# Transformer layer in split fp32: wide products on a [high|low] operand, loads of x between the weight loads, wider empty products

## The chip, the cores and the metric

The kernel runs on one core of a Trainium2 chip. The metric is the device time of one execution in microseconds; of several runs the median is given. TensorE multiplies (its products read a stationary tile of 128 columns and stream a moving operand of up to 512), VectorE, ScalarE and GpSimd (POOL) work element by element, and the queues of SyncE (SP), ScalarE and GpSimd issue DMA transfers.

## The reference

One decoder layer on 256 tokens of width 2048: a hybrid mixer (a windowed attention with sinks and a native sparse attention), a cross-attention to 256 memory tokens, a squared-ReLU MLP, each with a residual and a layer norm.

```python
h = x @ w_in                                  # 2048 x 7216
(q_a, k_a, v_a, q_b, k_c, v_c, k_s, v_s, k_w, v_w, g_nsa, g_merge) = jnp.split(h, offsets, axis=-1)
y_a = swa_sink_attention(...); y_b = nsa_attention(...)
mix = (sigmoid(g_a) * (y_a @ w_branch_swa) + sigmoid(g_b) * (y_b @ w_branch_nsa)) @ w_mix_out
h = layer_norm(DN_ALPHA * x + mix, ln1_g, ln1_b)
xa = memory_cross_attention(h, mem, xa_w_q, xa_w_kv, xa_w_o)
h = layer_norm(DN_ALPHA * h + xa, ln2_g, ln2_b)
ff = jnp.square(jax.nn.relu(h @ mlp_w1)) @ mlp_w2       # 2048 -> 8192 -> 2048
out = layer_norm(DN_ALPHA * h + ff, ln3_g, ln3_b)
```

## The kernel before

All large matmuls are computed in a split form: each fp32 operand is written as a high part (rounded by the cast to fp32r) and a low part (the rest), and a product is high by high, high by low and low by high, three TensorE products into one sum. Activations are kept transposed, 16 tiles k of 128 features by 256 tokens, as two tensors, one of high parts and one of low parts (`xth`/`xtl` for x, `mth`/`mtl` for the merged mixer, `meth`/`metl` for memory, `h1th`, `h2th` and their low parts after the norms).

The weights come in *chunks* of 512 KB (1024 columns by 128 partitions), a list that `run_chunks` goes through in order. `emit_load` issues a chunk's DMAs on the SP queue into one of five `raw` buffers, `emit_splits` makes the high part `h` on ScalarE (line 168) and the low part `l` on VectorE (line 169), up to three chunks ahead, and the chunk's `mm` issues the products. Between chunks, `side.phase` lets side jobs (attention heads, transpositions, norms) take one step on TensorE ("pe") or on the others ("ev"). A block is the set of chunks that adds into the same PSUM banks; after its last chunk `post` issues the copies that empty the banks (`evac`). Blocks have two forms:

- `block_x` (activations stationary, weights moving, 512 columns): `mm_x`, lines 201 to 208. The gates, the branches, the mixer output, the second MLP matmul (`mlp_w2`).
- `block_w` (weights stationary, 256 tokens moving): `mm_w`, lines 216 to 219, three products 256 wide for each 128 columns of weight. The two query blocks of `w_in` (1024 columns each), the keys of the memory, the queries of the cross-attention (512 each) and the first MLP matmul `mlp_w1` (8 blocks of 1024 columns). Two 128-column results lie in one bank. Blocks use the four banks "acc"; in the first MLP matmul every other block uses four others (`alt`).

The first 16 chunks (`make_c`, key/value stage) are mixed: 432 value and gate columns as `mm_x`, five 128-column key groups as `mm_w`. Their columns lie apart in `w_in`, so each chunk is five DMAs (`kv_loads`). x itself is loaded in columns: 0 to 256 and 256 to 512 on SP around the first chunk, the rest as three loads of 512 columns from the GpSimd queue, after four small tables; `x_side` transposes 256 columns (line 1215) after each of the first chunks. Behind the key/value stage come the swa query block with eight small chunks of the compression MLP between its chunks (`make_cmp`), then the nsa query block; `compress` (lines 541 to 573) is the rest of the compression MLP, a chain of small steps on VectorE and TensorE. After a query block `evac_q` copies the banks to `qraw`, from where `stack_q` makes the operands of the heads.

`keep_warm` issues products of a zero tile that nobody reads; it is called once, with 20 products of 128 columns, in `after_wo`, just ahead of the norm that precedes the MLP.

## Time and profile before

| | |
|---|---|
| median of 3 runs | 1442.91 us (1441.77 to 1443.74) |
| profiled execution | 1444.05 us, span 1442.3 us |
| busy | PE 98%, VectorE (DVE) 61%, ScalarE (ACT) 49%, POOL 12% |
| products (MATMUL) | 8732 |
| HBM read | 264.97 MB, 185 GB/s over the span |
| stages, about | key/value 7 to 68 us, queries to 196, gates, branches, mixer to 597, cross-attention to 708, first MLP matmul to 1081, second to 1427, last norm to 1442 |

The busy time of an engine is the union of its instructions. A product shows its whole way through the array, so the next one starts before it ends; the distance from start to start is what a train of products costs. In a timeline, brackets give the idle time of the engine before the instruction and what ended it.

### The profile page before, as it was taken

To read this page: it belongs to the slowest core of one execution; us is meant where nothing else is said; L and a number is where in the kernel's file an instruction comes from. 1 tells how busy PE (TensorE), PEld (TensorE's weight loads), DVE (VectorE), ACT (ScalarE), POOL (GpSimd) and SP (SyncE) were. 2 spreads that over 40 slices of the span, in tenths; PEclk is the share of its full clock that TensorE was granted. 3 is DMA by queue.
4 is the path that set the end of the run, shared out by engine and by line. 5 is a ranking of instruction groups with operands and counts; after the bars stand their busy time and mean duration, and the time that the engine had idled before them with its cause. 6 is when DMAs were issued, how large, how long until landed. Compare 5 with 4: busy or idle time off the path is not lost.

```text
span 1442.3 us, 22448 instructions
## 1 busy us (share of the span) xinstructions
PE 1412.6 (98%) x8732; PEld 1275.6 (88%) x8732; DVE 875.2 (61%) x1323; ACT 712.0 (49%) x1098; POOL 174.5 (12%) x165
## 2 busy tenths in 40 slices
PE   7999999999999999999999999999999999999996
PEld 6999988888888888899899999999998888888885
DVE  3577887888546466675854444444446555665556
ACT  3465776677444444454444444344445544544452
POOL 3002221221001010130201111011101000000002
PEclk9999999999999999999999999999999999999998
DMA  8765555454766575574355555665657666566552
GB/s 232 228 209 186 161 150 172 146 149 132 248 192 186 190 292 184 164 239 144 132 180 186 180 184 178 190 182 184 183 183 250 193 197 191 176 212 195 192 193 84
DMA packets 96282, 268.58 MB, mean 186 GB/s; under 512 B 9344, under 2 KB 32592, under 8 KB 95408
## 3 DMA queue, kind: packets, MB, share of 16 engines
q1 hardware_dynamic: 93344, 254.71, 56.5%
q0 software_dynamic: 2832, 12.45, 2.5%
q8 instruction: 68, 1.11, 0.3%
q14 instruction: 38, 0.31, 0.1%
HBM read 264.97 MB, written 2.15 MB: 185 GB/s over the span
## 4 chain that ended last, share of the span: by engine, by line
PE 66%; issue 25%; DVE 5%; ACT 2%; POOL 1%; DMA 1%; SPq 0%; ACTq 0%; DVEq 0%; POOLq 0%
PE acc L208 22%; PE acc L216 11%; PE acc L218 11%; PE acc L219 11%; DVE l L169 2%; PE acc L201 1%; PE acc L203 1%; PE acc L202 1%; DMA raw<-in_w_in_dram 1%; PE pt L662 1%; DVE p L635 1%; PE tr L337 0%; PE hid L528 0%; PE ntr L955 0%; PE o L671 0%
## 5 line engine op out<-in xcount | busy, mean ns | idle before, releaser
L169 DVE TENSOR_TENSOR l<-raw,h 128x1024 fp32r<-128x1024 f32 (+2 forms) x469 | 590.5, 1263 | 474.5 <-ACT h L168 466.3
L168 ACT CAST h<-raw 128x1024 fp32r<-128x1024 f32 (+2 forms) x469 | 490.2, 1048 | 534.6 <-PE acc L208 255.8
L216 PE MATMUL acc<-h2th,h 128*128 128x256 f32 x1024 | 291.3, 284 | 0.0
L218 PE MATMUL acc<-h2tl,h 128*128 128x256 f32 x1024 | 290.7, 284 | 0.0
L219 PE MATMUL acc<-h2th,l 128*128 128x256 f32 x1024 | 290.6, 284 | 0.0
L216 PEld LDWEIGHTS acc<-h2th,h 128*128 128x128 f32 x1024 | 197.6, 193 | 0.0
L218 PEld LDWEIGHTS acc<-h2tl,h 128*128 128x128 f32 x1024 | 197.5, 193 | 0.0
L219 PEld LDWEIGHTS acc<-h2th,l 128*128 128x128 f32 x1024 | 197.5, 193 | 0.0
L208 PE MATMUL acc<-l,ah 128*128 128x512 f32 x476 | 146.6, 389 | 0.0
L208 PE MATMUL acc<-h,ah 128*128 128x512 f32 x476 | 146.5, 389 | 0.0
L208 PE MATMUL acc<-h,al 128*128 128x512 f32 x476 | 146.5, 389 | 0.0
L208 PEld LDWEIGHTS acc<-l,ah 128*128 128x128 f32 x476 | 89.3, 188 | 18.6
L208 PEld LDWEIGHTS acc<-h,al 128*128 128x128 f32 x476 | 89.3, 188 | 18.6
L208 PEld LDWEIGHTS acc<-h,ah 128*128 128x128 f32 x476 | 89.3, 188 | 18.5
L216 PE MATMUL acc<-xth,h 128*128 128x256 f32 x336 | 97.5, 290 | 0.1
L219 PE MATMUL acc<-xth,l 128*128 128x256 f32 x336 | 96.7, 288 | 0.0
L218 PE MATMUL acc<-xtl,h 128*128 128x256 f32 x336 | 96.7, 288 | 0.0
L208 PE MATMUL acc<-h,xth 128*128 128x512 f32 (+1 forms) x252 | 81.2, 394 | 3.5 <-ACT h L168 3.5
L1148 POOL TENSOR_TENSOR a<-relu 128x512 f32<-128x512 f32 x32 | 44.3, 1412 | 314.6 <-ACT relu L1146 314.6
L208 PE MATMUL acc<-l,xth 128*128 128x512 f32 (+1 forms) x252 | 79.7, 388 | 0.6 <-DVE l L169 0.6
L208 PE MATMUL acc<-h,xtl 128*128 128x512 f32 (+1 forms) x252 | 79.5, 387 | 0.0
L216 PEld LDWEIGHTS acc<-xth,h 128*128 128x128 f32 x336 | 66.5, 198 | 0.6 <-ACT gt L483 0.2
(304 smaller groups left out, 2139.8 us busy)
## 6 DMA issues: line engine op xcount, KB each, us to landing
raw<-in_mlp_w_dram SPq DMA_DIRECT2D x256, 512.0 KB, 4.1
raw<-in_w_in_dram SPq DMA_DIRECT2D x96, 512.0 KB, 3.6
raw<-in_w_mix_out_dram SPq DMA_DIRECT2D x32, 512.0 KB, 4.2
raw<-in_w_branch_swa_dram SPq DMA_DIRECT2D x16, 512.0 KB, 3.6
raw<-in_w_branch_nsa_dram SPq DMA_DIRECT2D x16, 512.0 KB, 3.6
raw<-in_xa_w_kv_dram SPq DMA_DIRECT2D x16, 512.0 KB, 4.4
raw<-in_w_in_dram SPq DMA_DIRECT2D x48, 128.0 KB, 2.8
tbias<-udram POOLq DMA_DIRECT2D x8, 512.0 KB, 4.9
```

What stands on the lines that cost most here:

```text
L168: nc.scalar.copy(h[:, c0:c1], raws[c][:, c0:c1])
L169: nc.vector.tensor_sub(l[:, c0:c1], raws[c][:, c0:c1], fp(h[:, c0:c1]))
L201: nc.tensor.matmul(a, lhsT=xh(s), rhs=h[:, c0:c1], start=first, stop=False)
L202: nc.tensor.matmul(a, lhsT=xh(s), rhs=l[:, c0:c1], start=False, stop=False)
L203: nc.tensor.matmul(a, lhsT=xl(s), rhs=h[:, c0:c1], start=False, stop=last)
L208: nc.tensor.matmul(acc[s, b], lhsT=lhs(s), rhs=rhs[:, c0:c1], start=False, stop=False)
L216: nc.tensor.matmul(a, lhsT=h[:, c], rhs=xh, start=first and (t % 2 == 0 if opens is None else t in opens), stop=False)
L218: nc.tensor.matmul(a, lhsT=h[:, c], rhs=xl, start=False, stop=False)
L219: nc.tensor.matmul(a, lhsT=l[:, c], rhs=xh, start=False, stop=last and (t % 2 == 1 if closes is None else t in closes))
L635: nc.vector.tensor_tensor_reduce(p[:, c:c + w], lg[:, c:c + w], tbias[n.u][:, h, :w][:, ::-1], 1.0, -3e38, OP.add, OP.max, mx[:, i:i + 1])
L662: nc.tensor.transpose(pt[:, i * P:(i + 1) * P], p[:, b * P:(b + 1) * P], ident)
L1148: nc.gpsimd.tensor_mul(box["a"][k // KD][:, k % KD:k % KD + 2, :], two(r), two(r))
```

## The change

1. The high and low parts of a transposed activation now lie beside each other, [k][high|low][256 tokens], in two tiles of eight k each (class `Parts`); `both(k)` is a 512-column operand. The slots of the operands and of `qraw`, `yt` are renumbered accordingly.
2. `block_b` takes the place of `block_w` for the query blocks, the memory keys, the cross-attention queries and 14 half blocks of the first MLP matmul (its first 1024 columns stay `block_w`). Blocks are 512 columns wide, a chunk holds two k. Per 128 columns and k there is one product 512 wide (high weight by [high|low]) and one 256 wide (low weight by high). Each result tile fills a bank, whose halves `halves` adds (ScalarE copy, then VectorE add). In the MLP the square of the ReLU goes from POOL to VectorE.
3. The key/value chunks are three DMAs, 816 columns in one piece, and their split is in three parts (four for the first chunk), which also reorder the columns. x comes in pieces of 256 columns, the first on ScalarE's queue, the others between the chunks on SP; the small tables come on SP behind chunks 5 to 7.
4. `keep_warm` products are 512 wide. There are 5 ahead of the first transpositions and 4 behind them, and 8 instead of 20 before the last norm but one. `x_side` pauses one chunk between transpositions from the third on; `small_start` starts four steps later.

```diff
+class Parts:
+    def __init__(self, *tiles):
+        self.tiles = list(tiles)
+    def part(self, i, k0, k1):
+        return self.tiles[k0 // 8][:, k0 % 8:(k1 - 1) % 8 + 1, i, :]
+    def __call__(self, k):
+        t = self.tiles[k // 8][:, k % 8]
+        return t[:, 0, :], t[:, 1, :]
+    def both(self, k):
+        return self.tiles[k // 8][:, k % 8].rearrange("p i s -> p (i s)")
...
-                nc.tensor.matmul(ps[:, :P], lhsT=idle, rhs=idle, start=True, stop=True)
+                nc.tensor.matmul(ps.rearrange("p (a n) -> p a n", a=4), lhsT=idle,
+                                 rhs=idle.unsqueeze(1).to_broadcast([P, 4, P]), start=True, stop=True)
...
-            for c0, c1 in ((512, ch.n), (0, 512)) if c == 0 else ((0, ch.n),):
-                nc.scalar.copy(h[:, c0:c1], raws[c][:, c0:c1])
-                nc.vector.tensor_sub(l[:, c0:c1], raws[c][:, c0:c1], fp(h[:, c0:c1]))
+            for src, dst in ch.parts:
+                nc.scalar.copy(dst(h), src(raws[c]))
+                nc.vector.tensor_sub(dst(l), src(raws[c]), fp(dst(h)))
...
+    def block_b(w, n0, rhs, evac, tags=("acc",) * 4, pre=None):
+        box = {}
+        for k0 in range(0, KD, 2):
+            def mm(h, l, k0=k0):
+                if k0 == 0:
+                    box["t"] = [bank(tag, "acc") for tag in tags]
+                for a in range(2):
+                    k = k0 + a
+                    for t, o in enumerate(box["t"]):
+                        c = slice((4 * a + t) * P, (4 * a + t + 1) * P)
+                        nc.tensor.matmul(o, lhsT=h[:, c], rhs=rhs.both(k), start=k == 0, stop=False)
+                        nc.tensor.matmul(o[:, :S], lhsT=l[:, c], rhs=rhs(k)[0], start=False, stop=k == KD - 1)
...
+    def halves(dst, t, scale=None):
+        if scale is None:
+            nc.scalar.copy(dst, t[:, S:])
+            nc.vector.tensor_add(dst, t[:, :S], dst)
...
-    load_x(0, 256)
+    nc.scalar.dma_start(out=xraw[:, :, :S], in_=x[:, :S].rearrange("(s p) n -> p s n", p=P))
...
-    for c in range(512, D, 512):
-        load_x(c, c + 512, nc.gpsimd)
...
+        own = [(lambda r: r[:, 128:944], rows[:, COL_KC:COL_KC + 816]),
+               (lambda r: r[:, 0:128], rows[:, COL_KA:COL_KA + 128]),
+               (lambda r: r[:, 944:1072], rows[:, COL_VA:COL_VA + 128])]
+        pieces = {1: (1,), 2: (2,), 3: (3,), 4: (4,), 6: (5,), 8: (6,), 10: (7,)}.get(k, ())
+        more = [x_piece(m) for m in pieces] + small.get(k, [])
+        more = [(lambda r, t=t: t, src) for t, src in more]
+        return more + own if k == 1 else own + more
...
-    block_w(w_in, COL_QA, 1024, xk, evac_qa)
+    block_b(w_in, COL_QA, xk, lambda tiles: evac_q(0, 0, tiles))
+    evac_first.add(len(chunks) - 1)
+    block_b(w_in, COL_QA + 512, xk, evac_qa)
...
-    block_w(xa_w_kv[0], 0, 512, mek, evac_t("kt", None))
+    block_b(xa_w_kv[0], 0, me, evac_t("kt", None))
...
-        keep_warm(20, "mi")
+        keep_warm(8, "mi")
...
+    def evac_b(f):
+        def evac(tiles):
+            for b, t in enumerate(tiles):
+                r = box["pc"].tile([P, S], F32, tag="sum", name="sum", bufs=3)
+                halves(r, t)
+                k = 4 * f + b
+                nc.vector.scalar_tensor_tensor(box["a"][k // KD][:, k % KD, :], r, 0.0, r, op0=OP.max, op1=OP.mult)
...
-    for f in range(8):
-        block_w(mlp_w1[0], 1024 * f, 1024, hk, evac_a(f), tags=alt if f % 2 else ("acc",) * 4)
+    block_w(mlp_w1[0], 0, 1024, hk, evac_a(0))
+    for f in range(2, 16):
+        block_b(mlp_w1[0], 512 * f, hk, evac_b(f), tags=("acc",) * 4 if f % 2 else alt)
...
+    keep_warm(5, "mi")
+    for g in transpose_pairs(xraw, xk, range(1), "pt"):
         pass
+    keep_warm(4, "mi")
```

The SP queue at the start of the program, before (`raw_130`, `raw_137` are the buffers of chunks 0 and 1; a wait on DMAHW is one for an earlier load of the queues):

```order
L353 DMA xraw_88<-in_x_dram 128x2x256
L151 DMA raw_130<-in_w_in_dram 128x2x128
L151 DMA raw_130<-in_w_in_dram 128x256
L151 DMA raw_130<-in_w_in_dram 128x2x128
L151 DMA raw_130<-in_w_in_dram 128x128
L151 DMA raw_130<-in_w_in_dram 128x176
L353 DMA xraw_88<-in_x_dram 128x2x256
L151 DMA raw_137<-in_w_in_dram 128x2x128
L151 DMA raw_137<-in_w_in_dram 128x256 [waits DMAHW0_49]
L151 DMA raw_137<-in_w_in_dram 128x2x128 [waits DMAHW1_49]
```

and after the change, where `raw_116`, `raw_120`, `raw_125` are chunks 0, 1 and 2 (the first piece of x is now on ScalarE's queue):

```order
L170 DMA raw_116<-in_w_in_dram 128x816
L170 DMA raw_116<-in_w_in_dram 128x128 x2
L170 DMA xraw_88<-in_x_dram 128x2x256
L170 DMA raw_120<-in_w_in_dram 128x816
L170 DMA raw_120<-in_w_in_dram 128x128 x2
L170 DMA raw_125<-in_w_in_dram 128x816 [waits DMAHW0_49]
L170 DMA raw_125<-in_w_in_dram 128x128 [waits DMAHW1_49]
L170 DMA raw_125<-in_w_in_dram 128x128 [waits DMAHW2_49]
L170 DMA xraw_88<-in_x_dram 128x2x256 [waits DMAHW3_49]
```

Chunk 0 is no longer behind the first piece of x, the second piece stands ahead of chunk 1, the third behind chunk 2; the five loads of a chunk are three.

TensorE at the end of the swa query block and the start of the nsa query block, before (`hidt` is a step of the compression MLP, `acc_754` the last bank of the old block, `acc_1412` the first of the new one):

```order
L216 MATMUL acc_754<-xth_89,h_1291 128x256
L218 MATMUL acc_754<-xtl_90,h_1291 128x256
L219 MATMUL acc_754<-xth_89,l_1292 128x256
L549 MATMUL hidt_1387<-early_92 128x32 [waits Activation_49,Pool_49]
L549 MATMUL hidt_1387<-early_92 128x32
L549 MATMUL hidt_1388<-early_92 128x32 [waits DVE_49,Pool_49]
L549 MATMUL hidt_1388<-early_92 128x32
L216 MATMUL acc_1412<-xth_89,h_1305 128x256 [waits Activation_49]
L218 MATMUL acc_1412<-xtl_90,h_1305 128x256
L219 MATMUL acc_1412<-xth_89,l_1306 128x256
L216 MATMUL acc_1412<-xth_89,h_1305 128x256
```

and after the change (`xt1_90` and `xt0_89` hold the [high|low] pairs of k 8 to 15 and 0 to 7):

```order
L307 MATMUL acc_1042<-xt1_90,h_1240 128x512
L308 MATMUL acc_1042<-xt1_90,l_1241 128x256
L307 MATMUL acc_1043<-xt1_90,h_1240 128x512
L308 MATMUL acc_1043<-xt1_90,l_1241 128x256
L612 MATMUL hidt_1323<-early_92 128x32 [waits Activation_49,Pool_49]
L612 MATMUL hidt_1324<-early_92 128x32 [waits DVE_49,Pool_49]
L307 MATMUL acc_1348<-xt0_89,h_1254 128x512 [waits DVE_49]
L308 MATMUL acc_1348<-xt0_89,l_1255 128x256
L307 MATMUL acc_1349<-xt0_89,h_1254 128x512 [waits DVE_49]
L308 MATMUL acc_1349<-xt0_89,l_1255 128x256
L307 MATMUL acc_1350<-xt0_89,h_1254 128x512 [waits DVE_49]
```

Three 256-wide products have become a 512-wide and a 256-wide one, and the new block's first product of each bank waits for VectorE, where it waited for ScalarE on the first bank; the banks follow each other every second product instead of every sixth.

TensorE at the start of the program, after the change (before, its first rows were the four transpositions `tr` and then line 201's products of chunk 0):

```order
L141 MATMUL warm_140<-idle_69 128x512 [waits DVE_49]
L141 MATMUL warm_140<-idle_69 128x512 x4
L387 MATMUL tr_146<-ident_71,xraw_88 128x128 [waits DMAHW0_49,Pool_49]
L387 MATMUL tr_146<-ident_71,xraw_88 128x128 x3
L141 MATMUL warm_153<-idle_69 128x512 [waits PE_49]
L141 MATMUL warm_153<-idle_69 128x512 x3
L566 MATMUL acc_191<-h_158,xt0_89 128x432 [waits Activation_49]
L567 MATMUL acc_191<-h_158,xt0_89 128x432 [waits DVE_49]
```

Empty products stand ahead of the first transpositions and between them and chunk 0.

## Rows read from the trace of the kernel before

**Rows 1.** The page's busy times: engine, busy us, share of the span, instructions.
```profile
PE 1412.6 (98%) x8732; PEld 1275.6 (88%) x8732; DVE 875.2 (61%) x1323; ACT 712.0 (49%) x1098; POOL 174.5 (12%) x165
```
**Rows 2.** TensorE's groups by shape: line, engine, operation, shapes, count, busy us, mean ns.
```profile
L216 PE MATMUL acc<-h2th,h 128*128 128x256 f32 x1024 | 291.3, 284 | 0.0
L216 PE MATMUL acc<-xth,h 128*128 128x256 f32 x336 | 97.5, 290 | 0.1
L216 PE MATMUL acc<-meth,h 128*128 128x256 f32 x64 | 18.5, 289 | 0.0
L216 PE MATMUL acc<-h1th,h 128*128 128x256 f32 x64 | 18.1, 283 | 0.0
```
**Rows 3.** First MLP matmul: us, busy (x) PE, PEld, DVE, ACT, POOL, clock, DMA, GB/s.
```profile
830.00:930.00 100.00, 100.00 (x836) 100.00 (x835) 43.02 (x36) 41.02 (x43) 11.12 (x8) 1.00 0.60 182
```
**Rows 4.** Timeline of PE (start, us, operation), in the first and the second MLP matmul.
```profile
801.07 0.28 PE L219 MATMUL acc<-h2th,l 128*128 128x256 f32 x1
801.19 0.28 PE L216 MATMUL acc<-h2th,h 128*128 128x256 f32 x1
...
1200.52 0.61 PE L208 MATMUL acc<-h,al 128*128 128x512 f32 x2
1201.88 0.61 PE L208 MATMUL acc<-h,al 128*128 128x512 f32 x2
```
**Rows 5.** Timeline of PE at the last key/value chunk, 432 columns followed by 256.
```profile
66.34 0.36 PE L203 MATMUL acc<-h,xtl 128*128 128x432 f32 x1
66.54 0.28 PE L216 MATMUL acc<-xth,h 128*128 128x256 f32 x1
66.66 0.28 PE L218 MATMUL acc<-xtl,h 128*128 128x256 f32 x1
```
**Rows 6.** Timeline at the start: first product, split and products of chunk 1, chunk 2.
```profile
7.34 0.73 PE L201 MATMUL acc<-h,xth 128*128 128x432 f32 x1 [2.50 <-ACT h L168]
...
16.03 1.08 ACT L168 CAST h<-raw 128x1072 fp32r<-128x1072 f32 x1 [8.22 <-DMA raw<-in_w_in_dram]
...
17.17 0.73 PE L208 MATMUL acc<-h,xth 128*128 128x432 f32 x1 [3.50 <-ACT h L168]
...
23.74 0.44 PE L208 MATMUL acc<-h,xth 128*128 128x432 f32 x1
```
**Rows 7.** Stretches of 2 us at the start, columns as in rows 3.
```profile
0.00:2.00 2.00, 0.00 (x0) 0.00 (x0) 0.25 (x4) 1.26 (x1) 1.39 (x8) 1.00 0.04 12
...
10.00:12.00 2.00, 2.00 (x10) 1.97 (x10) 0.00 (x0) 0.00 (x0) 0.73 (x1) 1.00 1.02 355
...
20.00:22.00 2.00, 2.00 (x10) 1.94 (x10) 0.21 (x1) 0.00 (x0) 0.00 (x0) 0.50 0.87 219
```
**Rows 8.** Timeline at the end of the swa query block: copies out of banks, next block.
```profile
119.89 0.37 ACT L541 COPY early<-hid 128x256 f32<-128x256 f32 x1
...
121.11 0.59 ACT L310 COPY qraw<-acc 128x512 f32<-128x512 f32 x1
121.15 0.42 DVE L542 COPY early<-hid 128x256 f32<-128x256 f32 x1
...
123.23 0.39 PE L216 MATMUL acc<-xth,h 128*128 128x256 f32 x1
```
**Rows 9.** Timeline of DVE at the end of the key/value stage.
```profile
69.30 0.56 DVE L323 TENSOR_TENSOR vs<-acc,vs 128x384 fp32r<-128x384 f32 x1 [1.07 <-ACT vs L322]
69.78 0.68 DVE L486 COPY early<-acc 128x512 f32<-128x512 f32 x1
```
**Rows 10.** TensorE's waits: who waited for whom, us in total, times, longest.
```profile
PE kvc L570 <- DVE early L561: 1.7, 1, 1.7
```
**Rows 11.** The norm ahead of the MLP: the empty products, then the stretch from 710 us.
```profile
702.22 2.34 PE L123 MATMUL warm<-idle 128*128 128x128 f32 x20
...
710.00:712.00 2.00, 2.00 (x11) 2.00 (x10) 1.47 (x3) 2.00 (x3) 1.08 (x2) 0.50 0.00 0
```

164 lines of the change are left out of this document (87 added, 77 removed).

## The prediction

> **What bounds the kernel now.** I read the busy table first, then the groups by shape, then TensorE's own order of time, and last the stretches where it stands still. TensorE is busy for 98% of the span [rows 1]; as busy says little for pipelined products, I took the distance from start to start. A product 256 columns wide starts 0.12 us after the one before it, and over 100 us of the first MLP matmul 836 of them run, with VectorE busy for 43 us of the 100 and ScalarE for 41 [rows 3, 4]. In the second MLP matmul, six products 512 columns wide go from 1200.52 to 1201.88, 0.2267 us each [rows 4]. At the full clock of 2.4 GHz, 256 and 512 columns alone would take 0.1067 and 0.2133 us, so both widths carry the same 0.0133 us on top: it goes with the product, not with the columns. Nearly all of the span is such a train; the engine really waits at three places only: the start, the little compression MLP at 130 us, and the norm at 705 us. So a change pays either in the number of products or in one of these places.
>
> **Part 1: wide products.** A 128-column weight tile against 256 tokens was three products of 256 columns (high by high, high by low, low by high). The change makes two: high by [high|low], 512 wide, and low by high. By the pitches a triple goes from 3 x 0.120 = 0.360 to 0.2267 + 0.120 = 0.3467 us, 13.3 ns less. How many triples: h2 had 1024, of which the first 1024 columns of w1 (8 tiles x 16 k = 128) keep the old form, leaving 896; the two query blocks have 16 tiles x 16 = 256 of the 336 on x, the other 80 being key/value products that stay; memory keys and cross-attention queries have 64 each [rows 2]. Together 1280, and 1280 x 13.3 ns = **-17.0 us**. No row shows the two widths in strict alternation; the nearest is a 432-wide product followed by 256-wide ones, where the steps are 0.20 and 0.12 us [rows 5], that is 432/2.4 GHz = 0.18 plus 0.02, then 0.1067 plus 0.013. The bounds are therefore 7 ns less (the step after the wide one is 0.20 instead of 0.193) and 13.3 ns a triple: -8.5 to -17 us. I take the upper end, since the wide products here are the 512 shape that already runs at 0.2267.
>
> The Trainium skill, "TensorE: Matmul & The Clock Gate", section "Back-to-back issue gap", speaks against this part: it gives an isolated gap of N/2.4 + 2.5 ns, so that a product saved is worth 2.5 ns and the whole part only 3.2 us. The pitches here disagree with it (13.3 ns at both widths), and the measurement decides.
>
> **Part 2: handing banks back.** The price of the new form is the end of a block. Half sums now lie side by side in a bank, so each 128-column tile needs a ScalarE copy (0.37 us for 256 columns) and a VectorE add (0.42) before its bank is free [rows 8]. Before, a bank was complete well ahead of the block's end: the copy of the first bank began at 121.11 and the next block's first product ran at 123.23 without a wait. Now a tile is complete only 4, 3, 2, 1 pairs before the end, 1.04 us for the first; its release takes about 0.2 + 0.37 + 0.15 + 0.42 = 1.15 us (0.2 and 0.15 are my estimates of the handshakes), and the other three follow at 0.42 where the products come at 0.35. That is some 0.3 us of waiting per end, if both engines are free, about 1.5 if a 1.2 us split is in front. In the first MLP matmul blocks alternate between two sets of four banks, so it hits no block but the last (the second matmul opens on the same four): 0.5. Ends on the same banks: first to second half of the swa queries has a compression chunk between (0); swa to nsa queries 0.5; half to half of the nsa queries 0.8; nsa queries to gates 0.3; memory keys to values and cross-attention queries to values 0.4 each. At the end of the key/value stage the second and third bank come free through VectorE ops that end at 69.85 and 70.46 [rows 9]; the first query block used them at its seventh and thirteenth product, 0.72 and 1.44 us in, and now wants them at 0.35 and 0.69: +1.2. Sum **+4.1 us**, bounds +1.5 and +9. The compression MLP then waits on VectorE (1.7 us there now [rows 10]) behind four adds of 0.42 instead of two copies of 0.6: **+0.6**, bounds 0 and +1. The extra adds in the first MLP matmul (8 ops of some 0.42 per 22 us, the squares having left POOL) are hidden: VectorE has 57% free there [rows 3]; if the cover failed, it would be 3 us for each of 14 blocks.
>
> **Part 3: the start.** Before, TensorE's first product runs at 7.34, but chunk 1 waits for its loads: ScalarE begins its split at 16.03, the products at 17.17; TensorE had stood still since 13.7, and the granted clock goes down to 0.50 (1.2 GHz), and chunk 2 starts at 23.74 [rows 6, 7]. In that time all of x and chunks 0 to 2 came in together. The change sends x in 256-column pieces between the chunks on one queue. A chunk is 128 x 1072 x 4 B = 0.55 MB, a piece 0.26 MB; nothing moves in the first 2 us, then 219 to 355 GB/s [rows 7]. The first piece and chunk 0 (0.81 MB) are in at 4.3 to 5.7, and the first product, behind transposition and a split in four pieces, runs at about 7.0. Chunk 1 and its piece (1.62 MB in all) are in at 6.6 to 9.4; chunk 2 and the third piece (2.43 MB) at 8.8 to 13.1. Chunk 0 then takes 3.0 us at the full clock (0.1067 + 0.013 for 15 products, 0.19 for 6) and 5.4 at half. Nine empty 512-wide products are set around the first transpositions, so TensorE is nearly always busy from 1 us on; I take half of chunk 0 as still slow: it ends at 11.2, four transpositions (0.4), chunk 1 from 11.6 to 14.6, four more, chunk 2 at 15.0. **-8.7 us** against 23.74; bounds: all fast, 13.9 (-9.8); loads at 219 GB/s and the clock late, 17.7 (-6.0). Splits in three pieces cost ScalarE and VectorE some 0.4 us more per chunk, hidden in 3 us; the later pieces and small tables come in while the same products run. The queue's own waits are for a load eight back, as before.
>
> **Part 4: the 20 empty products** before the last norm (2.34 us) become 8 wide ones (8 x 0.227 = 1.8): 0, as the transposition after them waits for the norm. The clock falls there now, to 0.50 at 710 [rows 11]; if it stays up, the products from 708 to 712 run at 0.12 instead of 0.21: -2 us, kept for the range.
>
> **Sum.** -17.0 + 4.1 + 0.6 - 8.7 = -21.0 us. The profiled execution took 1444.05 (span 1442.3), giving 1423.0; it lies 1.1 above the median of the three runs, 1442.91, so the forecast is **1422.0 us**. A difference of 0.2% (2.9 us) is about what a measurement can tell from none.
>
> **The rivals.** *The start stays.* The loads, not their order, bound it, and chunk 2 still begins near 23.7: 1442.9 - 17.0 + 4.7 = 1430.6. For it: 219 GB/s around 20 us; against: chunks 0 to 2 with three pieces are 2.4 MB, where before all of x (2.1 MB) was under way with them, 3.7 in all. 10%. *The products save little.* The fixed part belongs to the switch between widths or to the weights, and a triple stays near 0.358: 1442.9 - 3 + 4.7 - 8.7 = 1436. Against it stand two equal fixed parts at two widths. 5%. The rule of the Trainium skill given above would make it come out this way. Both at once, the change does nothing: 1442.9 - 3 + 4.7 = 1445, or 1443 with a better clock. 3%. *Slower: the narrow product cannot cover the next weights.* A weight load shows as 0.19 us and is hidden behind products that all have one width; if, in the alternation, the load behind each 256-wide product surfaced, the triple would be 0.2267 + 0.193 = 0.42 us, 60 ns more than now, and 1280 x 60 = 77 us: 1442.9 + 77 + 4.7 - 8.7 = 1516. It decides from 0.363 us a triple on, where it eats parts 2 and 3. Against it: the 256-wide train has its loads hidden at 0.12. 3%.
>
> **How the numbers follow.** The forecast, both gains, has 79%; its own range is 1415 (start 13.9, cheap ends, clock kept at the norm) to 1428 (start -6, ends +9 and some of part 1 lost). Taking in the rival of the start, the range is 1415 to 1431. Faster: 79 + 10 + 5 = 94, less 1 for a product rival with dear ends: 0.93. Same 0.04, slower 0.03.
>
> **What would show it.** In the new profile: 512- and 256-wide products of the first MLP matmul in pairs 0.347 us apart, some 575 products in 100 us; that matmul some 12 us shorter (896 x 13.3 ns); chunk 2 of the key/value stage at about 15 us, at the full clock; waits of products on VectorE's adds of a few tenths at each end on the same banks, 1.5 at the first. Wrong would be: a pair at 0.36 or more; chunk 1 still waiting for a load after 12 us; VectorE's splits ending TensorE's waits in the query blocks.

## The result and the profile after

The changed kernel takes 1430.35 us (median of 4 runs, 1429.42 to 1431.72), the kernel before, beside it, 1442.72 (1441.77 to 1443.74): a ratio of 0.9915, 95% interval 0.9898 to 0.9932. It is faster by 12.4 us. That lies inside the range of 1415 to 1431, at its edge; the forecast was 1422.0, so the gain is 8.4 us short of it. The forecast's own range ended at 1428, and 1430.35 is outside of that; the stretch up to 1431 had been taken in for the case that the start stays as it was, which did not come about. That the time lies inside is luck. The profiled execution is the quickest of the four, 1429.42 us with a span of 1427.6.

Busy times of the page of the changed kernel, and its groups of products in the first MLP matmul (line, engine, operation, names, shapes, count, busy us, mean ns). They answer to [rows 1, 2]:
```profile
PE 1400.0 (98%) x7449; PEld 1200.6 (84%) x7449; DVE 917.6 (64%) x1487; ACT 723.9 (51%) x1178; POOL 130.0 (9%) x123
...
L307 PE MATMUL acc<-h2t,h 128*128 128x512 f32 x896 | 316.6, 399 | 0.0
L308 PE MATMUL acc<-h2t,l 128*128 128x256 f32 x896 | 251.6, 281 | 0.0
```
There are 1283 fewer products, 1280 of them by the triples counted ahead and 3 by the empty products, and TensorE is still busy for 98%. What a product costs is not in these rows. It is in the stretch that answers to [rows 3] (us, then busy and count of PE, PEld, DVE, ACT, POOL, clock, DMA share, GB/s):
```profile
830.00:930.00 100.00, 100.00 (x568) 86.76 (x567) 56.07 (x69) 42.93 (x54) 0.00 (x0) 1.00 0.64 188
```
There are 568 products in 100 us, where the forecast wanted some 575. TensorE's order of time (start, us, operation), against [rows 4], shows the same from start to start:
```profile
830.07 0.40 PE L307 MATMUL acc<-h2t,h 128*128 128x512 f32 x1
830.31 0.28 PE L308 MATMUL acc<-h2t,l 128*128 128x256 f32 x1
830.43 0.40 PE L307 MATMUL acc<-h2t,h 128*128 128x512 f32 x1
830.66 0.28 PE L308 MATMUL acc<-h2t,l 128*128 128x256 f32 x1
```
Wide to narrow takes 0.23 or 0.24 us, narrow to wide 0.11 or 0.12. Over the stretch from 900 to 1050 us the mean distance from one wide product to the next is 353.3 ns: six products take 241, 120, 236, 113, 233 and 117 ns, 1060 ns for three pairs, and this pattern repeats without a fault. The old triple was 360.0, the forecast 346.7. Half of the 13.3 ns is there.

The start answers to [rows 6]:
```profile
1.06 2.50 PE L141 MATMUL warm<-idle 128*128 128x512 f32 x5 [1.06 <-DVE rowmask L147]
5.19 1.08 PE L387 MATMUL tr<-ident,xraw 128*128 128x128 f32 x4 [1.63 <-DMA xraw<-in_x_dram]
...
7.78 0.55 PE L566 MATMUL acc<-h,xt 128*128 128x432 f32 x1
8.14 0.39 PE L567 MATMUL acc<-h,xt 128*128 128x432 f32 x1
8.37 0.36 PE L566 MATMUL acc<-h,xt 128*128 128x432 f32 x1
8.56 0.35 PE L567 MATMUL acc<-h,xt 128*128 128x432 f32 x1
...
11.28 0.44 PE L227 MATMUL acc<-h,xt 128*128 128x432 f32 x1
...
14.65 0.44 PE L227 MATMUL acc<-h,xt 128*128 128x432 f32 x1
```
Chunk 1 waits for nothing, and chunk 2 starts at 14.65 instead of 23.74 (forecast 15.0). The clock is seen in the steps: 0.36 us for 432 columns (7.78 to 8.14) is 1.2 GHz, 0.19 (8.37 to 8.56) is 2.4. Waits of TensorE between 120 and 240 us (who waited for whom, us in total, times, longest), against [rows 10]:
```profile
PE kvc L633 <- DVE early L624: 3.0, 1, 3.0
PE o L737 <- DVE ptl L373: 1.4, 5, 0.3
PE o L736 <- ACT pth L372: 0.8, 2, 0.6
PE acc L220 <- DVE qraw L321: 0.8, 1, 0.8
```
In the kernel before, the second and third of these were 0.3 and nothing, the last nothing. But its compression MLP had a second wait, which is gone:
```profile
PE kvc L573 <- DVE early L564: 0.9, 1, 0.9
```
So TensorE waited 2.6 us there before (1.7 and 0.9) and waits 3.0 now. At the norm ahead of the MLP, two stretches (us, PE busy and count, clock, DMA share, GB/s), against [rows 11]: first the kernel before, then the changed one.
```profile
696.00:712.00 16.00, 14.32 (x75) 0.80 0.29 99
```
```profile
696.00:712.00 16.00, 13.40 (x107) 1.00 0.30 92
```

Put together by stage, from the first product of a stage to that of the next, in us:

| stage | before | changed | difference | forecast |
|---|---|---|---|---|
| to the first query product | 68.53 | 60.20 | -8.3 | -8.7 |
| first query block, to the compression MLP | 62.41 | 63.29 | +0.9 | |
| on to the first product on an attention output | 116.26 | 116.53 | +0.3 | |
| (both query stages) | 178.67 | 179.82 | +1.2 | 0.0 |
| on to the first MLP matmul | 460.81 | 459.73 | -1.1 | -0.9 |
| first MLP matmul | 373.26 | 366.29 | -7.0 | -11.9 |
| second MLP matmul and last norm | 361.0 | 361.6 | +0.6 | +0.5 |

The last column is the forecast's own terms, sorted by stage: -3.4 for 256 triples and +3.4 of waits in the queries, -1.7 and +0.8 in the cross-attention, -11.9 for 896 triples. They sum to its -21.0; the measured ones to -14.6, the difference of the two spans. The medians lie 2 us closer: the profiled execution of before is 1.3 us above the median that it is compared by, that of the changed kernel 0.9 below its own. Two stages are off: the first MLP matmul by 5 us, the queries by 1, and by more at an equal clock (see `e2_old_products`).

### The profile page after: what moved, and what is told of

It reads as the page before. It is cut to its first block, busy times and chain, and to the rows that moved or that the text cites. A ratio compares the mean times of both kernels' runs of the same rounds, so it can differ in the third digit from the quotient of the medians.

```text
span 1427.6 us, 19988 instructions
## 1 busy us (share of the span) xinstructions
PE 1400.0 (98%) x7449; PEld 1200.6 (84%) x7449; DVE 917.6 (64%) x1487; ACT 723.9 (51%) x1178; POOL 130.0 (9%) x123
## 4 chain that ended last, share of the span: by engine, by line
PE 64%; issue 26%; DVE 6%; ACT 2%; POOL 1%; DMA 0%; ACTq 0%; DVEq 0%; POOLq 0%
PE acc L227 22%; PE acc L307 18%; PE acc L308 9%; DVE l L188 2%; PE acc L235 2%; PE acc L237 1%; PE acc L238 1%; PE acc L220 1%; PE acc L221 1%; PE acc L222 1%; PE pt L728 1%; POOL res L1010 1%; PE tr L387 1%; DVE res L1009 1%; ACT h L187 0%
## 5 line engine op out<-in xcount | busy, mean ns | idle before, releaser
L188 DVE TENSOR_TENSOR l<-raw,h 128x1024 fp32r<-128x1024 f32 (+4 forms) x501 | 587.2, 1182 | 412.2 <-ACT h L187 406.0
L187 ACT CAST h<-raw 128x1024 fp32r<-128x1024 f32 (+4 forms) x501 | 493.5, 994 | 491.5 <-PE acc L227 253.5
L307 PE MATMUL acc<-h2t,h 128*128 128x512 f32 x896 | 316.6, 399 | 0.0
L308 PE MATMUL acc<-h2t,l 128*128 128x256 f32 x896 | 251.6, 281 | 0.0
L307 PEld LDWEIGHTS acc<-h2t,h 128*128 128x128 f32 x896 | 168.4, 188 | 41.9
L308 PEld LDWEIGHTS acc<-h2t,l 128*128 128x128 f32 x896 | 169.3, 189 | 0.0
L227 PE MATMUL acc<-h,xt 128*128 128x512 f32 (+1 forms) x504 | 143.5, 389 | 0.0
L227 PEld LDWEIGHTS acc<-h,xt 128*128 128x128 f32 x504 | 93.0, 188 | 16.3
L307 PE MATMUL acc<-xt,h 128*128 128x512 f32 x256 | 91.9, 400 | 1.4 <-ACT gt L538 1.4
L227 PE MATMUL acc<-l,xt 128*128 128x512 f32 (+1 forms) x252 | 79.2, 386 | 0.0
```

The costliest lines, as they stand in the source:

```text
L187: nc.scalar.copy(dst(h), src(raws[c]))
L188: nc.vector.tensor_sub(dst(l), src(raws[c]), fp(dst(h)))
L227: nc.tensor.matmul(acc[s, b], lhsT=lhs(s), rhs=rhs[:, c0:c1], start=False, stop=False)
L307: nc.tensor.matmul(o, lhsT=h[:, c], rhs=rhs.both(k), start=k == 0, stop=False)
L308: nc.tensor.matmul(o[:, :S], lhsT=l[:, c], rhs=rhs(k)[0], start=False, stop=k == KD - 1)
```

## The experiments

Each kernel is the changed one but for the edit shown (two start from the tile-outer kernel, and say so). Ratios are to the kernel before, with 95% intervals. These reach some 2 us to either side, so the medians alone do not settle a difference of 1 or 2 us between two kernels; where one is read here, it rests on the stages, of which each kernel has one profile.

### The start and the products apart

`e2_old_products` undoes the products and keeps the start:
```diff
-    block_w(mlp_w1[0], 0, 1024, hk, evac_a(0))
-    for f in range(2, 16):
-        block_b(mlp_w1[0], 512 * f, hk, evac_b(f), tags=("acc",) * 4 if f % 2 else alt)
+    for f in range(8):
+        block_w(mlp_w1[0], 1024 * f, 1024, hk, evac_a(f), tags=alt if f % 2 else ("acc",) * 4)
```
and in the same way for the queries, the keys and the cross-attention queries, with the old numbers of two small buffers.

> All blocks that the change made wide get the old three products of 256 columns again, with the old copies out of the banks; the start, the order of loads, the operand's layout and the empty products stay as changed. My theory: the start alone is worth 9.1 us (the second chunk at 14.65 instead of 23.74 us) and the clock kept before the last norm 0 to 2, so 1442.7 - 9.1 - 0 to 2 = 1431.6 to 1433.6 us; the wide products then net only 1 to 3 us of the change. Rival: the start's gain is partly lost again later and the products carry more, so this kernel is at 1436 us or above. The pitch in the first MLP matmul is 0.120 us and the clock falls or stays before the last norm as in the changed kernel if it depends on the empty products alone.

Measured: 1434.63 us, ratio 0.9945 (0.9930 to 0.9961). The start, with what else this kernel keeps, is thus worth 8.2 of the 12.4 us, and the products 4.3 net; the run lies between the theories, 1.0 above the one and 1.4 below the rival. By stage this kernel has 61.21 us to the first query product, then 62.65 and 114.84 (177.5 for the queries, 2.3 less than the changed kernel), and 372.81 in the first MLP matmul (6.5 more). Of the 6.5, 0.8 is the clock at the norm: the 384 products on the first 1024 columns, which are the same in both kernels, take 50.25 us here and 49.41 in the changed kernel. So the wide products gain some 5.7 us in the MLP and lose 2.3 in the queries. This is a fairer comparison of the queries than that with the kernel before: the clock column over 120 to 140 us is 0.91 in this kernel and in the changed one, but 0.83 in the kernel before. What that is worth is seen in e7, e8 and e11, which have the changed kernel's query blocks and 0.83: there the stretch after the compression MLP takes 118.1 us instead of 116.53, and the queries 181.4 instead of 179.82, 2.7 more than in the kernel before.

`e3_old_queries` undoes the query blocks alone.

> Only the two query blocks get the old three products back (1024 columns a block, 16 chunks each); memory keys, cross-attention queries and the first MLP matmul stay wide. In the changed kernel the stretch from the first query product to the gates is 1.1 us longer than before. Theory (the hand-back of banks after adds and the wait of the compression MLP eat the 1.7 to 3.4 us that the products bring there): the stretch goes back to 127.8 us, and the run is about 1.1 us faster than the changed kernel, near 1429.3. Rival (the stretch is longer for its layout or loads, not for the hand-back): it stays at 128.9 and with the products' gain undone rises to about 131, the run to 1432.

Measured: 1427.97 us, 0.9902 (0.9886 to 0.9918), 2.4 us below the changed kernel by the medians. The stretch from the first query product to that on an attention output is 178.96 us against 179.82, and 116.31 of it after the compression MLP, although the clock column over 120 to 140 us is 0.83 here. Against the changed query blocks at 0.83 (181.4 us) the old ones gain 2.4. The rival is out: old products are better in the queries, by more than the theory's 1.1.

### What a pair costs

Three kernels order the same products otherwise; W is a wide product, N a narrow one. The changed kernel runs WNWN.

`e1_grouped` (WWWWNNNN):
```diff
                     for t, o in enumerate(box["t"]):
                         c = slice((4 * a + t) * P, (4 * a + t + 1) * P)
                         nc.tensor.matmul(o, lhsT=h[:, c], rhs=rhs.both(k), start=k == 0, stop=False)
+                    for t, o in enumerate(box["t"]):
+                        c = slice((4 * a + t) * P, (4 * a + t + 1) * P)
                         nc.tensor.matmul(o[:, :S], lhsT=l[:, c], rhs=rhs(k)[0], start=False, stop=k == KD - 1)
```

> Per row of 128 k, the four wide products run first and then the four narrow ones, so the width changes twice in eight products instead of eight times; nothing else moves. The changed kernel runs a pair in 353.3 ns in the first MLP matmul where 346.7 was forecast. Theory A (the lost 6.7 ns sit in the change of width): a quarter of them is left, 348.4 ns a pair, the 896 pairs of the first MLP matmul save 4.4 us and the other blocks some 1 to 2 more, so the run takes about 1425 us against 1430.4. Theory B (the wide read of [high|low] itself starts its successor 233 ns later, whoever comes next): no change, 1430 us, and steps of 233 ns inside the wide four. Theory C (the pair's order locks TensorE's sequencer into a slow rhythm, seen as a fixed pattern 241, 236, 233 over three pairs): another order gives another rhythm, which may be 346.7 ns or worse than 353; the run is then 1424 or above 1431 us.

Measured: 1431.73 us, 0.9925 (0.9910 to 0.9940). The pair takes 350.8 ns in the first MLP matmul, which is 1.1 us shorter (365.19); but a block's four tiles now all end in its last 0.5 us, and the query stages take 181.1 us instead of 179.8. Theory A (348.4) and theory B (353.3) both miss the pitch.

`e4_tile_outer` (WWNN, tile by tile):
```diff
-                for a in range(2):
-                    k = k0 + a
-                    for t, o in enumerate(box["t"]):
+                for t, o in enumerate(box["t"]):
+                    for a in range(2):
+                        k = k0 + a
                         c = slice((4 * a + t) * P, (4 * a + t + 1) * P)
                         nc.tensor.matmul(o, lhsT=h[:, c], rhs=rhs.both(k), start=k == 0, stop=False)
+                    for a in range(2):
+                        k = k0 + a
+                        c = slice((4 * a + t) * P, (4 * a + t + 1) * P)
                         nc.tensor.matmul(o[:, :S], lhsT=l[:, c], rhs=rhs(k)[0], start=False, stop=k == KD - 1)
```

> Within a chunk the tiles are the outer loop: two wide and two narrow products for a tile, then the next tile. A bank is then complete 2.1, 1.4, 0.7 and 0 us before the block's end and wanted again 0, 0.7, 1.4, 2.1 us after its start; the width changes half as often. Hand-back theory: waits of block products on the adds (3.0 us before the compression MLP apart) go, some 3 us between the first query block and the gates. Theory A on the pitch: 350 ns, -3 us in the first MLP matmul; B: 353, no change there. Together A 1424.5 us, B 1427.5 us; if the hand-back is not the cause of the lost query gain, 1427.5 (A) or 1430.4 (B).

Measured: 1426.26 us, 0.9885 (0.9864 to 0.9905). 348.3 ns a pair, and the first MLP matmul takes 362.12 us, 4.2 less than in the changed kernel. From the first query product to the compression MLP it is 61.21 us instead of 63.29: the wait for the third bank (0.89 us in the changed kernel, see Part 2 below) has shrunk to 0.2, and the first wait of the compression MLP from 3.0 to 1.8. But after the compression MLP nothing is won (118.66 us with the clock column at 0.83, where the changed order takes 118.1 at 0.83), and the waits on the split probabilities stay at 2.2 us (rows below).

`e9_wnnw` keeps the tiles' order of the changed kernel but runs W0 N0 N1 W1 for each two tiles, so that the train is WWNN again.

> For each row of 128 k but the first the order is wide, narrow of tile 0, narrow, wide of tile 1, and the same for tiles 2 and 3: the train is wide, wide, narrow, narrow as in the tile-outer kernel, but the tiles complete one after another near the block's end as in the changed kernel. If the order of the widths sets the rhythm: 347.2 to 348.3 ns a pair, some 576 products in 100 us, the first MLP matmul 362 us instead of 366.3, the run 1425 to 1426.5 us (the waits at block ends stay). If the tile-outer kernel was fast for another reason (two products in a row into the same bank, or weights of one tile in a row): 353 ns, 568 products, 1430 us.

Measured: 1425.71 us, 0.9874 (0.9860 to 0.9889); 348.7 ns a pair, first MLP matmul 362.33 us. The order of the widths does it, not the two products in a row into one bank.

`e6_low_wide` makes both products of a pair wide:
```diff
-                        nc.tensor.matmul(o[:, :S], lhsT=l[:, c], rhs=rhs(k)[0], start=False, stop=k == KD - 1)
+                        nc.tensor.matmul(o[:, :lw], lhsT=l[:, c], rhs=rhs.both(k)[:, :lw], start=False, stop=k == KD - 1)
```

> From column 4096 of the first MLP matmul on, the product with the low weights is 512 columns wide too (low by [high|low], so low by low is added to the sum); order and everything else as in the changed kernel. 512 pairs become pairs of two wide products. If a wide product on fresh weights costs 233 ns by itself, a pair is 466 ns and the run 1430.4 + 512 x 0.113 = 1488 us. If only a mixed train has the extra 6.7 ns (by the change of width, or by a rhythm that the mixed order locks into), a pair is 2 x 226.7 = 453.3 ns and the run 1430.4 + 512 x 0.100 = 1482 us, and the steps are all 226 to 227 ns.

Measured: 1482.23 us, once. A pair takes 453.3 ns, every step is 226 or 227. A wide product on fresh weights costs no more than any other of 512 columns; theory B falls.

The rows behind these pitches, the same columns as in [rows 3], one fence each for e1, e4, e9 and e6:
```profile
830.00:930.00 100.00, 100.00 (x573) 87.38 (x572) 55.48 (x68) 42.06 (x52) 0.00 (x0) 1.00 0.62 188
```
```profile
830.00:930.00 100.00, 100.00 (x576) 87.25 (x576) 57.07 (x74) 44.02 (x56) 0.00 (x0) 1.00 0.62 189
```
```profile
830.00:930.00 100.00, 100.00 (x576) 87.32 (x575) 56.98 (x74) 44.53 (x56) 0.00 (x0) 1.00 0.63 188
```
```profile
900.00:1000.00 100.00, 100.00 (x443) 82.81 (x442) 42.47 (x52) 33.08 (x40) 0.00 (x0) 1.00 0.49 144
```
The counts of products are the point: 573, 576 and 576 against the changed kernel's 568, at the same clock and with VectorE under 60%; 443 in 100 us is what the uniform 512-column train of the second MLP matmul gives. Against the 346.7 ns that two uniform trains give, the excess of a pair is 6.7 ns with two changes of width in it (WNWN), 1.7 to 2.1 with one (WWNN), 4.2 with a half (WWWWNNNN), and 0 without (453.3, 360.0). It is not proportional to the changes, so it is no price per change; theory A falls too. Of the three theories C is left, a rhythm that goes with the order. That it is not the order alone is seen in the changed kernel itself. Its first query block runs the same WNWN order at 347 ns a pair (start to start 0.34 or 0.35 us):
```profile
62.52 0.40 PE L307 MATMUL acc<-xt,h 128*128 128x512 f32 x1
62.75 0.27 PE L308 MATMUL acc<-xt,l 128*128 128x256 f32 x1
62.86 0.40 PE L307 MATMUL acc<-xt,h 128*128 128x512 f32 x1
63.09 0.28 PE L308 MATMUL acc<-xt,l 128*128 128x256 f32 x1
63.21 0.39 PE L307 MATMUL acc<-xt,h 128*128 128x512 f32 x1
```
It does so until 83.7 us, where products of the compression MLP come in between, and is at 353 after them; four other kernels with this order (e6, e7, e8, e11) do the same at the same place.

`e10_kick` tries to provoke that, by one disturbance per chunk:
```diff
+                        if kick and k and a == t == 0:
+                            for i in range(2):
+                                nc.tensor.matmul(o[:, i * S:i * S + S], lhsT=h[:, c], rhs=rhs(k)[i], start=False, stop=False)
+                        else:
+                            nc.tensor.matmul(o, lhsT=h[:, c], rhs=rhs.both(k), start=k == 0, stop=False)
```

> In the blocks from column 4096 of the first MLP matmul on, one wide product in sixteen is made as two 256-column products under the same weights, which disturbs the train once in every 2.8 us; nothing else changes. In the columns before, the train stays at 353.3 ns a pair. If the order alone sets the rhythm, each disturbed chunk is eight pairs of 353.3 plus 13.3 ns, 2.84 us, and the 512 pairs take 0.9 us longer. If the same order has a fast and a slow rhythm and a disturbance can throw it from one into the other (the first query block of the changed kernel runs at 347 ns up to 83 us and at 353 after), part of the chunks are at 347 ns, 2.79 us, and the stretch gets shorter by up to 2.3 us in spite of the extra products.

Measured: 1431.02 us, once; the first MLP matmul takes 366.22 us. (The edit splits one wide product in eight, which is one product in sixteen.) In the disturbed part the mean pair, extra product included, is 352.6 ns; at the slow rhythm throughout it would be 353.3 plus 13.3 x 7/64 = 354.8. After some disturbances a few pairs run at 347 (steps of 230 and 117 ns), after most the pattern of 241, 236 and 233 is back. So the same order has both rhythms, and in this matmul it falls back to the slow one. This run shows it in another place too: its first query block, whose program is that of the changed kernel up to there, is at 353.4 ns from 68 to 85 us already, ahead of the compression MLP, where the changed kernel is at 346.7. So neither the order nor the interruption decides alone, and what makes the two rhythms was not found.

### The queries

`e5_tile_outer_qb_old` is the tile-outer kernel with the second query block old:
```diff
-    block_b(w_in, COL_QB, xk, lambda tiles: evac_q(1, 0, tiles), pre=lambda: side.require("stacks"))
-    evac_first.add(len(chunks) - 1)
-    block_b(w_in, COL_QB + 512, xk, evac_qb)
+    block_w(w_in, COL_QB, 1024, xk, evac_qb, pre=lambda: side.require("stacks"))
```

> The tile-outer order stays for the first query block, the keys, the cross-attention queries and the first MLP matmul; the second query block, which runs beside the softmax jobs, gets the old three products and copies back. Theory (beside those jobs VectorE is busy for over 80% of the time, and its adds out of the banks push back the splits of the probabilities, so that the products on them wait; the 1.7 us that the wide products can save there are lost on that): the waits of products on the split probabilities go from 2.2 us to about 0.3, the stretch from the compression MLP to the first product on an attention output goes from 116.5 us (changed kernel) to about 114.8 with the same 3.4 us of low clock or 116.3 with 6.8 us, and the run takes 1423 to 1425 us, below the tile-outer kernel's 1426.3. Rival (the block's products save time there as anywhere, and the waits only move): 1427.5 to 1428 us.

Measured: 1422.59 us, 0.9856 (0.9841 to 0.9871). This is the best version, 20.5 us below the kernel before it was run beside and 7.8 below the changed one. After the compression MLP it needs 115.78 us, 2.9 less than the tile-outer kernel, both with 0.83 in the clock column over 120 to 140 us. Its waits between 118 and 240 us, and then those of the tile-outer kernel between 120 and 240:
```profile
PE kvc L636 <- DVE early L627: 1.7, 1, 1.7
PE kvc L639 <- DVE early L630: 0.7, 1, 0.7
PE o L740 <- DVE ptl L376: 0.3, 1, 0.3
```
```profile
PE o L740 <- DVE ptl L376: 1.4, 5, 0.3
PE o L739 <- ACT pth L375: 0.8, 2, 0.6
PE acc L220 <- DVE qraw L324: 0.8, 1, 0.8
...
```
The three waits that go (1.4 less 0.3, 0.8, 0.8) are 2.7 us.

What happens at one of them is to be seen on ScalarE of the changed kernel, in the middle of that block (start, us, operation, idle time before):
```profile
148.33 1.43 ACT L320 COPY qraw<-acc 128x256 f32<-128x256 f32 x4 [1.90 <-PE acc L308]
149.66 1.05 ACT L187 CAST h<-raw 128x1024 fp32r<-128x1024 f32 x1
150.61 0.40 ACT L713 ACTIVATE p<-p,st 128x128 f32<-128x128 f32 x1
...
153.45 0.59 ACT L372 CAST pth<-pt 128x512 fp32r<-128x512 f32 x1
```
and on TensorE after it:
```profile
154.08 0.39 PE L736 MATMUL o<-pth,vs 128*128 128x256 f32 x1 [0.58 <-ACT pth L372]
154.81 0.38 PE L737 MATMUL o<-ptl,vs 128*128 128x256 f32 x1 [0.34 <-DVE ptl L373]
```
Four tiles leave their banks in the middle of the block, 1.43 us of copies, and the next weight split of 1.05 stands behind them; only then come the exponentials of the softmax job. Their probabilities are split at 153.45 to 154.04, but TensorE, whose place for the product on them is fixed by the chunks, is there at 153.5. In the kernel with old products a block empties its banks once, at its end. The same split and the same product in e2, on ScalarE and on TensorE:
```profile
153.11 0.59 ACT L372 CAST pth<-pt 128x512 fp32r<-128x512 f32 x1
```
```profile
155.40 0.28 PE L735 MATMUL o<-pth,vs 128*128 128x256 f32 x1
```
Counted from the first product behind the compression MLP's wait (123.49 in the changed kernel, 123.86 in e2), the split comes 0.7 us later here and TensorE 1.5 us earlier. So the wait at this product is made of both; the copies alone are not shown to be its cause.

`e12_qb_no_adds`, the tile-outer kernel again, asks whether it is the adds or the place. It leaves the sum of the high-by-low half out of the second query block, and with the four adds of a half block also two of ScalarE's four copies, as the rest is shared between ScalarE and VectorE:
```diff
-            halves(qraw[i][:, 4 * j + b, :], t)
+            if i == 1:
+                copy_any(qraw[i][:, 4 * j + b, :], t[:, :S])
+            else:
+                halves(qraw[i][:, 4 * j + b, :], t)
```

> The tile-outer kernel with another way out of the banks in the second query block: each tile's first half alone is copied by one engine, ScalarE and VectorE in turn, and the high-by-low half sums are left out there. Its two half blocks stay, with four tiles leaving in the middle of the block, but each leaves by 4 copies instead of 4 copies and 4 adds. If the extra adds are what delays the softmax jobs: the waits of products on the split probabilities fall from 2.2 us to 0.3 and the run takes 1423 to 1424.5 us, as with the old second block. If it is the place (tiles that leave in the middle of the block put the jobs' steps out of step with the chunks): the waits stay near 2 us and the run is at 1425.5 to 1426.5 us, as the tile-outer kernel.

Measured: 1423.99 us, 0.9863 (0.9846 to 0.9879). By its time the first theory holds, by its waits neither wholly:
```profile
PE o L743 <- DVE ptl L376: 1.4, 5, 0.3
...
PE o L742 <- ACT pth L375: 0.3, 1, 0.3
```
The waits for the first part of the split fall from 0.8 to 0.3 and that for the queries (0.8) goes, those for the second part stay at 1.4. After the compression MLP it takes 117.10 us: 1.6 of the 2.9 us go with the adds and the copies that are left out with them, which this run does not separate. The other 1.3 go with something else in the two half blocks; the place in the middle is the only candidate that was named, and it is not shown.

### The start

`e7_no_empty` leaves both groups of empty products at the start out (`keep_warm(5, "mi")` and `keep_warm(4, "mi")`).

> The nine empty products around the first transpositions are left out; loads and all else as changed. Theory (they make the clock rise at about 8.2 us): without them the clock rises only after some 5 us of products, near 13 us as in the kernel before, chunks 0 and 1 run half of their products at the low clock, the second chunk starts at 16 to 17.5 us instead of 14.65, and the run takes 1431.5 to 1433.5 us. Rival (the order of loads alone made the start): the second chunk at 14.7 to 15.2 us, the run within 0.5 us of 1430.4.

Measured: 1431.94 us, 0.9924 (0.9909 to 0.9939), 1.6 above the changed kernel.
```profile
7.70 0.73 PE L566 MATMUL acc<-h,xt 128*128 128x432 f32 x1 [1.32 <-ACT h L187]
8.22 0.56 PE L567 MATMUL acc<-h,xt 128*128 128x432 f32 x1
8.58 0.56 PE L566 MATMUL acc<-h,xt 128*128 128x432 f32 x1
...
13.83 0.44 PE L227 MATMUL acc<-h,xt 128*128 128x432 f32 x1
...
17.24 0.44 PE L227 MATMUL acc<-h,xt 128*128 128x432 f32 x1
```
From the second product on, chunk 0 runs in steps of 0.36 us for 432 columns, and chunk 2 starts at 17.24: in this execution, the longest of its four (1434.20 us), the empty products are worth 2.6 of the 9.1 us at this place. The other 6.5 belong to the order of the loads and to what was changed with it, the fewer DMAs of a chunk and its new split.

`e8_x_first` loads x ahead of chunk 1:
```diff
-        pieces = {1: (1,), 2: (2,), 3: (3,), 4: (4,), 6: (5,), 8: (6,), 10: (7,)}.get(k, ())
+        pieces = {1: range(1, 8)}.get(k, ())
```

> All seven later pieces of x are loaded between chunk 0 and chunk 1 instead of one ahead of every chunk or two; the empty products stay. Chunk 1 is then complete only after 0.81 + 1.84 + 0.55 = 3.2 MB, at 219 to 355 GB/s from 2 us on: 11.0 to 16.6 us. Theory (the order of the loads is what the start was bound by): chunk 1's products begin at 12.5 to 17.5 us instead of 11.3, the second chunk at 16 to 21, and the run loses 2 to 6 us: 1432.5 to 1436.5. Rival (TensorE is behind the loads anyway, once the clock is up): the second chunk stays at 14.7 to 15.5 us and the run at 1430.4.

Measured: 1435.06 us, 0.9938 (0.9921 to 0.9954), 4.7 above the changed kernel. Its order of time, and two of its stretches (us, PE busy and count, clock, DMA share, GB/s):
```profile
14.01 0.47 PE L227 MATMUL acc<-h,xt 128*128 128x432 f32 x1 [1.81 <-ACT h L187]
...
19.76 0.44 PE L227 MATMUL acc<-h,xt 128*128 128x432 f32 x1
```
```profile
12.00:14.00 2.00, 0.20 (x2) 1.00 1.05 390
...
16.00:18.00 2.00, 2.00 (x12) 0.55 0.87 292
```
Chunk 1 waits, TensorE stands still for two microseconds at 390 GB/s, and the clock falls behind the pause: the picture of [rows 6, 7] again. So the order bounds the start: it moves chunk 2 by 5.1 us here, in the longest of four executions that go from 1432.72 to 1436.69, and the run by 4.7 in the median. Some 1.4 of the 9.1 us are left that no run separates.

### The clock at the norm

`e11_norm_20` sets the 20 narrow empty products ahead of the norm again.

> The empty products ahead of the norm before the first MLP matmul are 20 of 128 columns again, as in the kernel before; those at the start stay 512 wide. In the profiles so far the clock fell there for 6.8 us with the 20 narrow ones, for 3.4 us or not at all with the 8 wide ones. If the empty products make that difference: 6.8 us at the low clock near 700 us, the run 0.7 to 2 us longer than the changed kernel, 1431 to 1432.5. If it is the moment at which the engine's pause falls: 0 to 3.4 us here too, and the run within 0.7 of 1430.4.

Measured: 1431.62 us, 0.9912 (0.9896 to 0.9929). In the same stretch of 16 us as above the clock is
```profile
696.00:712.00 16.00, 14.11 (x106) 0.89 0.24 70
```
The kernels with 8 wide ones have 1.00 there (the changed one, the best one) or 0.89 (e2, e4). So the form of the empty products did not decide; the 0.80 of before did not come back with them. The time, 1.3 us above the changed kernel, lies in the range of the first theory, but half of the low clock that this execution has more than the changed kernel's (6.8 us) lies at the compression MLP, far ahead of the edit (0.83 over 120 to 140 us). Whether the clock falls there differs between kernels that are alike at this place.

## Why the prediction was right, and where not

**Part 1, wide products: the failed step.** It took the upper end, 13.3 ns a triple, "since the wide products here are the 512 shape that already runs at 0.2267". The shape does run at that pitch among its like (453.3 ns for two, e6), so the ground was true, but it does not carry over to a mixed train: WNWN takes 353.3, 6.7 ns less than the old triple of 360.0. The price of 13.3 ns that goes with a product held in every uniform train; what the step left out is that a mixed train adds 6.7 ns of its own. 896 x 6.7 is 6.0 us, where 11.9 was taken; the stage shows -7.0, with 1.3 that the clock at the norm gave (its first 384 products take 49.41 us instead of 50.69) and 0.3 lost at its end. The text had this value as its lower bound, from [rows 5], the only rows with a mixed train: "7 ns less". With -8.5 for -17.0 the sum would have been 1430.5; that this is the measured time to 0.2 us is chance, as the profiled executions are 14.6 us apart, not 12.5, and the terms of the start and the queries are off as well. The ends were far apart, and the row nearest to the new order, that of a change of width, pointed to the lower one.

By the isolated gap that the Trainium skill, "TensorE: Matmul & The Clock Gate", section "Back-to-back issue gap", gives, a product saved would be worth an estimated 2.5 ns. The runs show 6.7 in the changed order and 11 to 12 in WWNN, so these trains do not agree with it; the rival it was named for (a triple near 0.358) is out as well.

**Part 2, the hand-back.** Forecast +4.1 and +0.6. TensorE at the first query block of the changed kernel (order of time, in brackets the wait):
```profile
60.20 0.50 PE L307 MATMUL acc<-xt,h 128*128 128x512 f32 x1 [0.52 <-ACT gt L538]
...
62.06 0.50 PE L307 MATMUL acc<-xt,h 128*128 128x512 f32 x1 [0.89 <-ACT gt L538]
```
The third bank (62.06) is wanted too early, as described (0.89 us, where 1.2 were taken for the block), though the profile puts the wait down to ScalarE's `gt` and not to VectorE; the opening one (60.20) waits as well, and does so with old products too (61.21 in e2, 0.52 us), so that this belongs to the new way of emptying the key/value banks. With old products the third bank is waited for too, by 0.18 us. The compression MLP waits 3.0 instead of 1.7, but its second wait of 0.9 is gone, so +0.4 (forecast +0.6). The handshakes of 0.2 and 0.15 us in the price of a release stood on no row. In the traces ScalarE starts 0.04 us after the end of the product that it waits for, and that end is 0.16 behind the product's pitch of 0.12 (it shows 0.28), which makes the 0.2; VectorE starts 0.03 after ScalarE, not 0.15. What was missed is that the second query block runs beside the softmax jobs, and that ScalarE and VectorE work there for TensorE too: 2.7 us of waits, of which half went in e12. The text named the rows that would tell ("VectorE's splits ending TensorE's waits in the query blocks" as a sign of being wrong), and they are there. Net, the queries lost 2.3 us where 0 was forecast. The waits add up to that: against e2, TensorE waits 0.7 us more for the banks at the first query block, 0.4 at the compression MLP, 1.9 on the split probabilities and 0.8 at the gates, 3.8 in all, and 256 pairs at 6.7 ns give 1.7 back.

**Part 3, the start.** -8.7 forecast, -9.1 at chunk 2 and -8.3 at the first query product. Both causes that it rests on are shown, the order of the loads (e8) and the empty products (e7). Its steps were less exact: the first product came at 7.78 us, not at about 7.0, and the clock was up at about 8.2, so that only the first product ran at the low pace where half of chunk 0 was taken. In most other kernels with the same start it rose later (in e2 only 5 products run between 9 and 10 us, 10 in the changed kernel), and the first query product comes at 60.3 to 61.7: a spread of a microsecond or so that is in every time here. The near hit of this term is in part the luck of this execution.

**Part 4, the norm.** 0, with -2 kept for the range. The stage differences show about 1 us in this profile; the clock in e11 says that it is not owed to the empty products' form.

**The rivals.** The start did not stay (23.74 against 14.65), no weight load surfaced by its 0.19 us (a pair takes 0.3533 where 0.42 was feared; whether the 6.7 ns that are missing have to do with the weights no run shows), and the change as a whole is not nothing (12.4 us).

## What to carry to other kernels

A pitch that was measured in a uniform train was the best case here for a mixed one; where the new order stands in no row, take the nearest mixed row or vary the order, since WWNN against WNWN was worth 4 us here. Ask of every engine that gets new work at a block's end which other jobs it serves at that moment: the same products gained in the MLP, where the blocks run alone, and lost in the second query block, which shares ScalarE and VectorE with a softmax. At a start that waits for loads, load what the first products need in the order of their use; the start was two thirds of the whole gain, and undoing the order alone lost 4.7 us.

## What was not expected of the hardware

Two trains with the same products in the same order run at 347 and at 353 ns a pair, each in a fixed pattern, for tens of microseconds and more (the first query block and the MLP of the changed kernel). In five kernels the first query block passes from 346.7 to 353.0 at the first products of the compression MLP, and in e10, with the same program up to there, it is at 353.4 ahead of them. The excess of a mixed train over its uniform parts was 6.7, 4.2 and 2 ns a pair for three orders, at the full clock in all of them. In the first 8 us the clock column reads 1.00 while 432 columns take 0.36 us, the pace of the lower level (1.2 GHz): the trace of the changed kernel has no clock entry before 8.2 us, and there the steps tell the clock, not the column.
